# Two batches of modulation and VectorE-only lower halves in a two-block transformer kernel

## The chip, the cores and the metric

The kernel runs on one core of one Trainium2 chip. The metric is the device time of one execution in microseconds; lower is better. The engines are named as the profile names them: PE (TensorE matmul) and PEld (its weight loads), DVE (VectorE), ACT (ScalarE), POOL (GpSimd) and SP (the queue that issues most DMAs).

## The reference, cut to what matters

Two transformer blocks follow each other on a sequence of 1024 tokens of width 1024, all in float32:

```python
def first_block(x, ...):
    h = rms_norm(x, norm_mix);  x = x + gated_deltanet(h, ...)      # 8 heads of 128
    x = x + squared_relu_mlp(rms_norm(x, norm_mlp), w_up, w_down)   # 1024 -> 4096 -> 1024
    return rms_norm(x, norm_final)

def second_block(x, c, ctx, c_ctx, w_mod, b_mod, ...):
    mx = split(silu(c) @ w_mod + b_mod, 6)          # six vectors of 1024
    mc = split(silu(c_ctx) @ w_mod + b_mod, 6)      # only the first two are used
    hx = modulate(rmsnorm(x, g_norm1), mx[0], mx[1])
    hc = modulate(rmsnorm(ctx, g_norm1), mc[0], mc[1])
    ...                                             # attention and gated linear attention
    x = x + mx[2] * (mixed @ w_out)
    x = x + mx[5] * swiglu(modulate(rmsnorm(x, g_norm2), mx[3], mx[4]), w_gu, w_down)
    return rmsnorm(x, g_final)
```

The modulation, `silu(c) @ w_mod`, is a product of one vector with a 1024 x 6144 matrix. It depends on none of the tokens, so it may be computed at any time before the second block's norms.

## The kernel before, in words

**Split operands.** Every large matrix product is done in three TensorE passes over rounded parts: an operand is copied to an upper half (`hi`, by ACT) and the rest is its lower half (`lo = raw - hi`, a subtraction with two inputs in SBUF). `wload` (L125 to L141) loads a weight tile, lets ACT make `whi` (L139) and either DVE or POOL make `wlo` (L140). In the DeltaNet stage POOL makes it for three of the four projections of each head (L274, L552: 24 tiles of 128x1024), DVE for the others.

**Stages, in the order of the trace.** (1) DeltaNet, in four pairs of heads. `project` (L272) does a 128x512 product per half of the tokens, then a causal convolution on DVE (L288 and three times L290), then a Silu on ACT (L292). Beside it DVE inverts triangular blocks row by row (L396, L400). (2) The output projection of heads 0 to 5 (L659 to L667): eight column blocks `o`, two halves of tokens each, 18 matmuls per half. A result leaves PSUM by DVE in the first half and by ACT in the second (L667). (3) `Up.half` and `Up.operands`: the residual (x transposed by PE, from tiles `xin2` that `out_tile` loads at L731), heads 6 and 7, the norm and the operands of the next stage. (4) The first MLP's `Up`: a Strassen scheme with seven products of 12 matmuls for each of 16 blocks `f`, 112 products; `evac` takes results from PSUM (L754), `spill` (from L1838) writes seven operand tiles per block to memory. (5) `Down`: four groups of 3, 4, 4 and 3 of those blocks, 28 products each. At a change of group seven sets of tiles `T` are loaded again and split by `Down.split` (L1893): ACT makes the upper half (L1898), DVE the lower half of every even tile and POOL that of every odd one (L1899). `prepare` makes weight sums on POOL (L1925 to L1930) and splits the block (L1934 on ACT, L1935 on DVE); a product's result is added to x on DVE (L1957). (6) A last group, the mixer of the second block and its output. (7) The second MLP in the same form: `Up` with 22 blocks, `Down` with three groups of 3 (its additions are L1959).

**The modulation.** `Modulation.stream` is a generator. It loads 128x512 tiles of `w_mod` (L873), multiplies each with one silu value per partition and adds it up on DVE (L884 for the first of eight tiles, L886 for the rest), then transposes and reduces the sum (L893, L895). There are twelve groups of eight tiles; groups 0 to 3 are done for two vectors, the others for one. `Modulation.finish` adds the rest up with four small PE products. Before the change groups 3 to 11 run in `Up`, one step after each product (`up.hook`, L775), with loads on SP's queue into the halves of x that are free there; groups 0 to 2 run in `Down`, one step after every second product from the 15th on (L799 to L801), with loads on POOL's queue.

**Order.** Each engine works through its own queue in order, and each DMA queue too. The program is written in Python order, but a scheduler places the instructions on each engine by the readiness that it expects, so the order on an engine need not be that of the text. Buffers of a pool tag are handed out again when their last reader is done; a new pool on memory of a closed one waits for the closed one's last readers.

Of the kernel before, what the change touches and what calls it, by code (L numbers as in the profile page):

```python
# [9 lines left out]
F32 = mybir.dt.float32  # L10
# [195 lines left out]
def deltanet(k, spill, dbg=None):  # L206

    nc, tc, A = k.nc, k.tc, k.A
    with ExitStack() as ctx:
# [62 lines left out]
        def project(h, part, out):  # L272

            W = k.wload(w_in[:, part * 1024 + h * 128: part * 1024 + h * 128 + 128], lo=nc.gpsimd if part != 1 else None)  # L274
# [276 lines left out]
        def gates(h, pr):  # L551
            W = k.wload(w_in[:, 3072 + h * 128:3072 + h * 128 + 128], lo=nc.gpsimd)  # L552
# [105 lines left out]

        x = []  # L659
# [8 lines left out]
        return gated, x  # L668
# [45 lines left out]
def dn_out_and_mlp(k, gated, mod, norms, cpd, x2d, ud, td):  # L714

    nc, A = k.nc, k.A
    x = k.x
    with ExitStack() as ctx:
# [47 lines left out]
        mod.open(P)  # L766
        ms = mod.stream(list(range(3, 12)), [x[f][:, 512:1024] for f in range(8)], nc.sync)
# [7 lines left out]
        up.hook = lambda: next(ms, None)  # L775
# [5 lines left out]
        ms = mod.stream(list(range(3)), [k.e() for _ in range(5)], nc.gpsimd)  # L781
# [11 lines left out]
        def hook(done, left):  # L793
            if left == 10:
                drain(ms)
                mod.finish()
# [50 lines left out]
class Modulation:  # L847
# [3 lines left out]
    def __init__(self, k):  # L851
# [5 lines left out]
        self.bm = k.vec["b_mod_2"]  # L857

    def open(self, P):
        nc, sc = self.k.nc, self.sc  # L860
        self.R = P.tile([128, 64, 4], F32, name="modR")
        nc.scalar.activation(sc[:, 0, :], self.k.vec["c_2"], AF.Silu)
        nc.scalar.activation(sc[:, 1, :], self.k.vec["c_ctx_2"], AF.Silu)

    def stream(self, groups, raws, q):
# [11 lines left out]
        for n, (g, j) in enumerate(todo):  # L877
            vs = range(2 if g < 4 else 1)
            if j == 0:
                accs = [k.e() for _ in vs]  # L880
# [9 lines left out]
            if j == 7:  # L890
                for v in vs:
                    tr = k.e()
                    nc.vector.transpose(tr, accs[v])  # L893
                    m = 48 * v + 4 * g
# [4 lines left out]
    def finish(self):  # L899

        k, nc, bm = self.k, self.k.nc, self.bm
        ps = k.pt((128, 64))
# [3 lines left out]
        nc.vector.tensor_tensor(out=k.mod, in0=ps[:, 0:48], in1=bm, op=ALU.add)  # L906
        nc.vector.tensor_tensor(out=k.modc, in0=ps[:, 48:64], in1=bm[:, 0:16], op=ALU.add)
# [712 lines left out]
class Up:  # L1620
# [112 lines left out]
    def run(self, upto=None):  # L1733

        while self.done < (upto or len(self.seq)):
# [126 lines left out]
class Down:  # L1862
# [267 lines left out]
def whole(ctx, tc, A, out):  # L2130
# [11 lines left out]
    with ExitStack() as c2:  # L2142
        k.xp = c2.enter_context(tc.tile_pool(name="xp", bufs=1, reuse_waits="tile"))
        k.s1 = c2.enter_context(tc.tile_pool(name="s1", bufs=16, reuse_waits="tile"))
        gated, k.x = deltanet(k, spill)
# [31 lines left out]
```

## Time and profile before

| what | us |
|---|---|
| median of three runs (lowest, highest) | 3005.15 (3001.58, 3014.09) |
| the profiled execution's own time | 3009.24 |
| its span from the first to the last instruction | 3007.2 |
| PE busy | 2804.1 (93%) |
| DVE busy | 2110.5 (70%) |
| ACT busy | 1404.8 (47%) |
| POOL busy | 799.6 (27%) |
| mean granted clock of PE | 0.978 |

PE is busy for nine tenths of the span, so what is lost are the stretches in which it waits and those after a wait in which it was granted the lower of its two clock levels. A share of busy time over the whole span tells little here; the stages differ, and each is read by itself.

### The profile page before, as it was taken

To read this page: it belongs to the slowest core of one execution; us is meant where nothing else is said; L and a number is where in the kernel's file an instruction comes from. 1 tells how busy PE (TensorE), PEld (TensorE's weight loads), DVE (VectorE), ACT (ScalarE), POOL (GpSimd) and SP (SyncE) were. 2 spreads that over 40 slices of the span, in tenths; PEclk is the share of its full clock that TensorE was granted. 3 is DMA by queue.
4 is the path that set the end of the run, shared out by engine and by line. 5 is a ranking of instruction groups with operands and counts; after the bars stand their busy time and mean duration, and the time that the engine had idled before them with its cause. 6 is when DMAs were issued, how large, how long until landed. Compare 5 with 4: busy or idle time off the path is not lost. (4 is left out here: it accounts for less than half of the span.)

```text
span 3007.2 us, 43812 instructions
## 1 busy us (share of the span) xinstructions
PE 2804.1 (93%) x16336; PEld 2284.9 (76%) x16336; DVE 2110.5 (70%) x3254; ACT 1404.8 (47%) x2685; POOL 799.6 (27%) x665
## 2 busy tenths in 40 slices
PE   7899989999899988899899998999899999999998
PEld 5777778787687867787777777788777788887777
DVE  5868686855988779877856667677757755556784
ACT  6343535333555553335633334677645433334345
POOL 1102020102133365542422222121120322334432
PEclk9999999999999999999999999999999999999999
DMA  4313131232577665442621111001033433335433
GB/s 110 58 28 73 27 81 31 58 120 99 162 236 230 204 227 177 141 139 73 185 68 41 48 50 45 12 29 60 15 126 106 133 102 100 97 115 173 132 105 109
DMA packets 330084, 310.16 MB, mean 103 GB/s; under 512 B 36640, under 2 KB 254720, under 8 KB 329872
## 3 DMA queue, kind: packets, MB, share of 16 engines
q1 hardware_dynamic: 277088, 220.90, 24.0%
q10 hardware_dynamic: 46480, 65.46, 6.0%
q0 software_dynamic: 6304, 21.01, 3.1%
q8 instruction: 128, 2.10, 0.3%
q14 instruction: 84, 0.69, 0.1%
HBM read 232.83 MB, written 74.48 MB: 102 GB/s over the span
## 5 line engine op out<-in xcount | busy, mean ns | idle before, releaser
L1709 PE MATMUL pt<-T,blk 128*128 128x512 f32 x608 | 244.8, 404 | 16.2 <-DVE e L754 8.4
L1711 PE MATMUL pt<-T,blk 128*128 128x512 f32 x608 | 244.7, 403 | 5.4 <-DVE blk L1698 5.4
L1710 PE MATMUL pt<-T,blk 128*128 128x512 f32 x608 | 244.5, 402 | 0.7 <-DVE T L1786 0.6
L139 ACT CAST whi<-wraw 128x1024 fp32r<-128x1024 f32 (+3 forms) x126 | 116.0, 920 | 221.9 <-PE pg L150 180.1
L149 PE MATMUL pg<-dhi,whi 128*128 128x512 f32 (+1 forms) x528 | 213.5, 404 | 2.1 <-ACT pre L285 1.8
L151 PE MATMUL pg<-dhi,wlo 128*128 128x512 f32 (+1 forms) x528 | 212.5, 402 | 1.5 <-POOL wlo L140 1.5
L150 PE MATMUL pg<-dlo,whi 128*128 128x512 f32 (+1 forms) x528 | 212.1, 402 | 1.1 <-DVE dlo L188 1.0
L1950 PE MATMUL pt<-T,blk 128*128 128x512 f32 x368 | 150.2, 408 | 29.4 <-DVE x L1957 19.7
L149 PE MATMUL pg<-xhi,whi 128*128 128x512 f32 x416 | 170.8, 410 | 1.4 <-ACT e L1024 1.4
L151 PE MATMUL pg<-xhi,wlo 128*128 128x512 f32 x416 | 167.4, 402 | 0.3 <-DVE wlo L140 0.3
L150 PE MATMUL pg<-xlo,whi 128*128 128x512 f32 x416 | 167.1, 402 | 0.0
L140 DVE TENSOR_TENSOR wlo<-wraw,whi 128x1024 fp32r<-128x1024 f32 (+3 forms) x101 | 110.0, 1090 | 74.6 <-ACT whi L139 69.8
L1709 PEld LDWEIGHTS pt<-T,blk 128*128 128x128 f32 x608 | 116.8, 193 | 48.1 <-ACT blk L1697 7.0
L1952 PE MATMUL pt<-T,blk 128*128 128x512 f32 x368 | 148.2, 403 | 1.4 <-DVE blk L1935 1.4
L1951 PE MATMUL pt<-T,blk 128*128 128x512 f32 x368 | 148.4, 403 | 0.0
L1711 PEld LDWEIGHTS pt<-T,blk 128*128 128x128 f32 x608 | 117.3, 193 | 33.6 <-DVE blk L1698 6.3
L1698 DVE TENSOR_TENSOR blk<-xb,blk 128x512 fp32r<-128x512 f32 x121 | 102.9, 851 | 54.9 <-ACT blk L1697 53.0
L1351 DVE TENSOR_TENSOR pl<-pt,ph 128x512 fp32r<-128x512 f32 x160 | 106.3, 683 | 47.2 <-ACT ph L1346 46.5
L1710 PEld LDWEIGHTS pt<-T,blk 128*128 128x128 f32 x608 | 117.1, 193 | 28.9 <-DVE T L1786 1.9
L1898 ACT CAST T<-T 128x512 fp32r<-128x512 f32 x161 | 96.1, 618 | 89.0 <-DMA T<-td 44.2
L1934 ACT CAST blk<-T 128x384 fp32r<-128x384 f32 (+1 forms) x133 | 71.8, 540 | 138.2 <-PE pt L1952 83.1
L1697 ACT CAST blk<-xb 128x512 fp32r<-128x512 f32 x121 | 74.2, 621 | 116.3 <-PE pt L1711 46.9
(570 smaller groups left out, 8273.2 us busy)
## 6 DMA issues: line engine op xcount, KB each, us to landing
x<-w_mod SPq DMA_DIRECT2D x72, 256.0 KB
wraw<-w_in SPq DMA_DIRECT2D x35, 512.0 KB
T<-td SPq DMA_DIRECT2D x69, 256.0 KB
wraw<-dn_w_in SPq DMA_DIRECT2D x32, 512.0 KB
td<-e ACTq DMA_DIRECT2D x55, 256.0 KB
xb<-w_gu SPq DMA_DIRECT2D x44, 256.0 KB
wraw<-w_gu SPq DMA_DIRECT2D x22, 512.0 KB
xin<-x SPq DMA_DIRECT2D x16, 512.0 KB
```

The lines of the kernel that those rows point to most:

```text
L139: nc.scalar.copy(hi, raw)
L140: (lo or nc.vector).tensor_tensor(out=lo_t, in0=raw, in1=hi, op=ALU.subtract)
L149: nc.tensor.matmul(out, hi[:, w, :], Hhi[k][:, sl], start=first and k == 0, stop=False)
L150: nc.tensor.matmul(out, hi[:, w, :], Hlo[k][:, sl], start=False, stop=False)
L151: nc.tensor.matmul(out, lo[:, w, :], Hhi[k][:, sl], start=False, stop=last and k == n - 1)
L1351: nc.vector.tensor_tensor(out=pl, in0=ps, in1=ph, op=ALU.subtract)
L1709: nc.tensor.matmul(ps, w[:, 0, j], T[j][:, 0], start=not c and j == 0, stop=False, skip_group_check=c)
L1710: nc.tensor.matmul(ps, w[:, 0, j], T[j][:, 1], start=False, stop=False, skip_group_check=c)
L1711: nc.tensor.matmul(ps, w[:, 1, j], T[j][:, 0], start=False, stop=j == 3, skip_group_check=c)
L1950: nc.tensor.matmul(ps, w[:, 0, j], T[j][:, 0], start=not c and j == 0, stop=False, skip_group_check=c)
L1951: nc.tensor.matmul(ps, w[:, 0, j], T[j][:, 1], start=False, stop=False, skip_group_check=c)
L1952: nc.tensor.matmul(ps, w[:, 1, j], T[j][:, 0], start=False, stop=j == n - 1, skip_group_check=c)
```

## The change

1. The `lo` argument that sent 24 lower halves of DeltaNet weights to POOL goes; DVE makes all of them.
2. The modulation is split in two. Groups 0 to 2 are streamed between the products of DeltaNet's output projection, two steps after each half, from buffers of DeltaNet's own pool (tags `k` and `dec`) with loads on POOL's queue, and get a `finish` of their own at the end of that stage. The vectors that they need are loaded ahead of that stage, on ACT's queue instead of SP's. Groups 3 to 11 stay in `Up`, but start after 24 products. Nothing of the modulation is left in `Down`.
3. `Down.split` has DVE make every lower half, in both MLPs.
4. In `Up.run` a product's result is taken from PSUM before `Down.start` is called, not after.

```diff
 def project(h, part, out):
-            W = k.wload(w_in[:, part * 1024 + h * 128: ...], lo=nc.gpsimd if part != 1 else None)
+            W = k.wload(w_in[:, part * 1024 + h * 128: ...])
 def gates(h, pr):
-            W = k.wload(w_in[:, 3072 + h * 128:3072 + h * 128 + 128], lo=nc.gpsimd)
+            W = k.wload(w_in[:, 3072 + h * 128:3072 + h * 128 + 128])
 # deltanet, output projection
+        k.load_vecs(VECS[1:], nc.scalar)
+        mod = Modulation(k)
+        mod.open(P, [0, 1, 2])
+        raws = [P.tile([128, 2, 512], F32, tag="k", name=k.nm("mraw"), bufs=4) for _ in range(4)]
...
+                t = P.tile([128, 2, 512], F32, tag="dec", name=k.nm("macc"), bufs=2)
...
+        ms = mod.stream([0, 1, 2], [t[:, j] for t in raws for j in range(2)], nc.gpsimd, tmp)
         for o in range(8):
...
                 (nc.scalar.copy if i else nc.vector.tensor_copy)(x[o][:, sl], ps)
+                next(ms, None)
+                next(ms, None)
+        drain(ms)
+        mod.finish()
 # dn_out_and_mlp
-        up.hook = lambda: next(ms, None)
+        up.hook = lambda: next(ms, None) if up.done > 24 else None
...
         drain(chain(ms, back(HALVES[0])))
-        ms = mod.stream(list(range(3)), [k.e() for _ in range(5)], nc.gpsimd)
+        mod.finish()
...
             if left == 10:
-                drain(ms)
-                mod.finish()
                 u.append(last_group(k, s1, "s1", ud[28:32]))
...
-            elif left > 10:
-                if done > 14 and done % 2 == 0:
-                    next(ms, None)
-            else:
+            elif left < 10:
 # Up.run
             r = self.product(f, m)
+            if r:
+                self.evac(f, *r)
             if f == self.n - 1 and self.after:
                 self.after(m)
-            if r:
-                self.evac(f, *r)
 # Down.split
-            (nc.gpsimd if j % 2 else nc.vector).tensor_tensor(out=t[:, 1], in0=t[:, 1].bitcast(F32), in1=t[:, 0], op=ALU.subtract)
+            nc.vector.tensor_tensor(out=t[:, 1], in0=t[:, 1].bitcast(F32), in1=t[:, 0], op=ALU.subtract)
```

How it moves instructions, at three places. **DVE in the output projection** (`x<-pg` takes a result of column block o from PSUM, `wlo` is the lower half of a later block's weights, `macc` and `modR` belong to the modulation). Before, from the end of the scan on:

```order
L140 TENSOR_TENSOR wlo_6251<-wraw_6249,whi_6250 128x768
L549 TENSOR_TENSOR ol_5826<-z_5680,oh_5825 128x512
L667 COPY x_6201<-pg_6208 128x512
L140 TENSOR_TENSOR wlo_6298<-wraw_6296,whi_6297 128x768
L667 COPY x_6248<-pg_6255 128x512
L140 TENSOR_TENSOR wlo_6345<-wraw_6343,whi_6344 128x768
L667 COPY x_6295<-pg_6302 128x512
```

With the change, in the same place; the last row here is the lower half for block 4, and the row `wlo_6323` for block 3 stands five rows above the first one:

```order
L900 SCALAR_TENSOR_TENSOR macc_6166<-mraw_6130,sc,macc_6166 128x512 x4
L680 COPY x_6258<-pg_6265 128x512
L907 STREAM_TRANSPOSE macc_6285<-macc_6166 128x512 x2
L909 TENSOR_REDUCE modR_6126<-macc_6285 128x16 x2
L898 TENSOR_SCALAR macc_6290<-mraw_6127,sc 128x512 x2
L900 SCALAR_TENSOR_TENSOR macc_6290<-mraw_6127,sc,macc_6290 128x512 x2
L900 SCALAR_TENSOR_TENSOR macc_6290<-mraw_6128,sc,macc_6290 128x512 x2
L680 COPY x_6320<-pg_6327 128x512
L900 SCALAR_TENSOR_TENSOR macc_6290<-mraw_6128,sc,macc_6290 128x512 x2
L900 SCALAR_TENSOR_TENSOR macc_6290<-mraw_6129,sc,macc_6290 128x512 x4
L900 SCALAR_TENSOR_TENSOR macc_6290<-mraw_6130,sc,macc_6290 128x512 x2
L140 TENSOR_TENSOR wlo_6382<-wraw_6380,whi_6381 128x768
```

Between `wlo_6323` and `wlo_6382` there now stand 34 instructions of the modulation and two copies; before, one copy stood between two lower halves.

**SP's queue at the end of the output projection** (`xin` are the x tiles of the residual, `dn_w_out` and `mlp_w_up` weights; in brackets the semaphores that a load waits for, `DMASW` being those of POOL's loads). Before:

```order
L138 DMA wraw_6296<-dn_w_out 128x6x128 [waits DMAHW3_49,DVE_49]
L731 DMA xin_1224_6536<-x 128x1024 [waits PE_49]
L138 DMA wraw_6343<-dn_w_out 128x6x128 [waits DMAHW4_49,DVE_49]
L731 DMA xin_1225_6538<-x 128x1024 [waits PE_49]
L731 DMA xin_1226_6540<-x 128x1024
L731 DMA xin_1227_6542<-x 128x1024
L731 DMA xin_1248_6687<-x 128x1024
L138 DMA wraw_6390<-dn_w_out 128x6x128 [waits DMAHW5_49,DVE_49]
```

With the change:

```order
L138 DMA wraw_6611<-dn_w_out 128x2x512 [waits DMAHW0_49,DVE_49]
L138 DMA wraw_6617<-dn_w_out 128x2x512 [waits DMAHW1_49,DVE_49]
L1680 DMA wraw_6893<-mlp_w_up 128x8x128 [waits DMAHW2_49,DVE_49]
L748 DMA xin_1236_6640<-x 128x1024 [waits DMASW6_49,DMASW5_49,DMASW7_49,DMASW0_49,PE_49]
L748 DMA xin_1237_6642<-x 128x1024 [waits PE_49]
L748 DMA xin_1238_6644<-x 128x1024
L748 DMA xin_1239_6646<-x 128x1024
```

The x tiles lie on memory that the modulation now uses to the end of the stage. They moved behind all weights of the output projection and the first weight of `Up`; the first waits for the modulation's last loads, and the PE count that the second waits for is raised by the four products of `finish`, which stand behind the last product of the projection.

**DVE in the first MLP's `Down`**, shortly after its start (`x<-x,ps` adds a product to x, `blk` is a weight block's lower half, `T` a tile's lower half, L884 and L886 modulation). Before:

```order
L1957 TENSOR_TENSOR x_6154<-x_6154,ps_9595 128x512
L1935 TENSOR_TENSOR blk_9607<-T_6529,blk_9607 128x384
L884 TENSOR_SCALAR e_9787<-e_9525,sc 128x512
L884 TENSOR_SCALAR e_9788<-e_9525,sc 128x512
L1957 TENSOR_TENSOR x_6248<-x_6248,ps_9611 128x512
L1935 TENSOR_TENSOR blk_9623<-draw_9334,blk_9623 128x384
L886 SCALAR_TENSOR_TENSOR e_9787<-e_9526,sc,e_9787 128x512
L886 SCALAR_TENSOR_TENSOR e_9788<-e_9526,sc,e_9788 128x512
```

With the change:

```order
L1972 TENSOR_TENSOR x_6258<-x_6258,pg_9684 128x512
L1950 TENSOR_TENSOR blk_9696<-T_6632,blk_9696 128x384
L1914 TENSOR_TENSOR T_7045<-T_7045 128x512
L1972 TENSOR_TENSOR x_6199<-x_6199,ps_9699 128x512
L1914 TENSOR_TENSOR T_7046<-T_7046 128x512
L1950 TENSOR_TENSOR blk_9711<-T_6633,blk_9711 128x384
L1914 TENSOR_TENSOR T_6630<-T_6630 128x512
L1972 TENSOR_TENSOR x_6320<-x_6320,ps_9715 128x512
```

The modulation's instructions are gone from between the additions, and every tile's lower half (odd and even numbers) stands on DVE.

## Rows read from the trace of the kernel before

**Rows 1.** The page, part 1: busy time and share of the span.
```profile
PE 2804.1 (93%) x16336; PEld 2284.9 (76%) x16336; DVE 2110.5 (70%) x3254; ACT 1404.8 (47%) x2685; POOL 799.6 (27%) x665
```

**Rows 2.** Stretches, us; busy us (count) per engine; granted clock; DMA share; GB/s.
```profile
70.00:620.00 550.00, 507.39 (x3556) 421.59 (x3554) 412.35 (x882) 247.84 (x662) 71.72 (x64) 0.98 0.24 53
620.00:703.00 83.00, 82.97 (x435) 70.02 (x434) 34.13 (x72) 23.16 (x57) 0.00 (x0) 1.00 0.28 94
...
1062.00:1091.00 29.00, 25.64 (x104) 20.16 (x102) 15.13 (x21) 20.05 (x39) 16.15 (x17) 0.94 0.99 345
1091.00:1235.00 144.00, 127.78 (x526) 100.78 (x525) 138.84 (x181) 51.09 (x94) 75.83 (x65) 0.96 0.50 161
1235.00:1395.00 160.00, 153.73 (x669) 123.40 (x667) 121.36 (x171) 66.74 (x122) 67.83 (x49) 0.98 0.36 120
2345.00:2735.00 390.00, 390.00 (x1681) 316.87 (x1681) 215.22 (x280) 140.39 (x240) 125.40 (x90) 1.00 0.34 111
2735.00:2942.00 207.00, 193.57 (x814) 155.69 (x813) 163.22 (x222) 83.31 (x156) 82.83 (x67) 0.98 0.40 130
```

**Rows 3.** PE's waits, 1091 to 1395 us: total, times, longest (us).
```profile
PE pt L1950 <- DVE x L1957: 19.7, 6, 6.0
```

**Rows 4.** Timeline of PE: the longest of those waits, at a change of group.
```profile
1248.69 0.76 PE L1950 MATMUL pt<-T,blk 128*128 128x512 f32 x1 [6.01 <-DVE x L1957]
```

**Rows 5.** DVE by form, 1060 to 1400 us: count, busy, mean ns, idle.
```profile
L1899 DVE TENSOR_TENSOR T<-T 128x512 fp32r<-128x512 f32 x56 | 59.2, 1067 | 16.9 <-ACT T L1898 16.9
...
L886 DVE SCALAR_TENSOR_TENSOR e<-e,sc,e 128x512 f32<-128x512 f32 x42 | 37.8, 927 | 0.0
```

**Rows 6.** Single lines, duration ns min/median/max: splits (both MLPs), modulation, additions.
```profile
L1899 DVE TENSOR_TENSOR T<-T x98: 644/692/1814, 1067.0 to 2887.7; 128x512 fp32r<-128x512 f32 x98
...
L1899 POOL TENSOR_TENSOR T<-T x63: 1262/1601/1862, 1067.7 to 2887.3; 128x512 fp32r<-128x512 f32 x63
...
L886 DVE SCALAR_TENSOR_TENSOR e<-e,sc,e x42: 736/740/1784, 1109.7 to 1217.0; 128x512 f32<-128x512 f32 x42
...
L1957 DVE TENSOR_TENSOR x<-x,pt x64: 643/675/689, 1091.2 to 1394.6; 128x512 f32<-128x512 f32 x64
```

**Rows 7.** Timeline of DVE and of POOL at the same change of group.
```profile
1239.44 3.49 DVE L1899 TENSOR_TENSOR T<-T 128x512 fp32r<-128x512 f32 x2
...
1238.93 1.75 POOL L1899 TENSOR_TENSOR T<-T 128x512 fp32r<-128x512 f32 x1
```

**Rows 8.** PE's waits, 785 to 1062 us (the first Up).
```profile
PE pt L1709 <- DVE e L754: 6.0, 2, 5.9
```

**Rows 9.** The stretch right after that long wait; columns as in rows 2.
```profile
807.00:816.00 9.00, 9.00 (x29) 7.16 (x30) 9.00 (x14) 4.14 (x8) 3.58 (x2) 0.71 0.78 262
```

**Rows 10.** PE's longest waits in DeltaNet, 70 to 620 us.
```profile
PE pt L468 <- ACT qT L292: 22.6, 9, 4.7
```

**Rows 11.** DeltaNet: POOL's lower halves by form; a DVE record beside one at 279.2.
```profile
L140 POOL TENSOR_TENSOR wlo<-wraw,whi 128x1024 fp32r<-128x1024 f32 x23 | 56.2, 2445 | 107.7 <-ACT whi L139 80.5 <-PE ps L524 16.9 <-PE pg L151 10.3
...
279.74 2.14 DVE L396 TENSOR_TENSOR pm<-X,A 64x252 f32<-64x252 f32 x1
```

**Rows 12.** DVE's groups by form, 620 to 703 us (output projection).
```profile
L667 DVE COPY x<-pg 128x512 f32<-128x512 f32 x8 | 5.5, 692 | 19.6 <-PE pg L151 19.6
...
L140 DVE TENSOR_TENSOR wlo<-wraw,whi 128x1024 fp32r<-128x1024 f32 x2 | 2.4, 1221 | 3.5 <-PE pg L151 3.5
```

**Rows 13.** Timeline: SP's first residual load; ACT on the kernel's first x tiles.
```profile
642.13 0.34 SPq L731 DMA_DIRECT2D xin<-x  x1
...
4.99 1.06 ACT L175 ACTIVATE xj<-xin 128x1024 f32<-128x1024 f32 x1 [0.81 <-DMA xin<-x]
...
7.99 1.06 ACT L175 ACTIVATE xj<-xin 128x1024 f32<-128x1024 f32 x1 [0.46 <-DMA xin<-x]
```

**Rows 14.** PE's waits, 2735 to 2942 us (second Up's end, second Down).
```profile
PE pt L1950 <- DVE xb L1959: 9.6, 2, 5.0
PE pt L1709 <- DVE e L2036: 3.7, 1, 3.7
```

More of the change, by code (lines that the diff above doesn't have):

```diff
@@ L272, in project @@
         def project(h, part, out):
-            W = k.wload(w_in[:, part * 1024 + h * 128: part * 1024 + h * 128 + 128], lo=nc.gpsimd if part != 1 else None)
+            W = k.wload(w_in[:, part * 1024 + h * 128: part * 1024 + h * 128 + 128])
             n = part * 8 + h
@@ L657, in deltanet, with tmp @@
                 values(p + 1)
+        k.load_vecs(VECS[1:], nc.scalar)
+        mod = Modulation(k)
+        mod.open(P, [0, 1, 2])
+        raws = [P.tile([128, 2, 512], F32, tag="k", name=k.nm("mraw"), bufs=4) for _ in range(4)]
+        tmps = []
+        def tmp():
+            if not tmps:
+                t = P.tile([128, 2, 512], F32, tag="dec", name=k.nm("macc"), bufs=2)
+                tmps.extend((t[:, 0], t[:, 1]))
+            return tmps.pop(0)
+        ms = mod.stream([0, 1, 2], [t[:, j] for t in raws for j in range(2)], nc.gpsimd, tmp)
         x = []
@@ L667, in deltanet @@
                 (nc.scalar.copy if i else nc.vector.tensor_copy)(x[o][:, sl], ps)
-        return gated, x
+                next(ms, None)
+                next(ms, None)
+        drain(ms)
+        mod.finish()
+        return gated, x, mod
 HALVES = [slice(0, 512), slice(512, 1024)]
@@ L765, in dn_out_and_mlp @@
         up.operands(out_tile)
-        mod.open(P)
-        ms = mod.stream(list(range(3, 12)), [x[f][:, 512:1024] for f in range(8)], nc.sync)
+        mod.open(P, list(range(3, 12)))
+        ms = mod.stream(list(range(3, 12)), [x[f][:, 512:1024] for f in range(8)], nc.sync, k.e)
         def back(h):
@@ L857, in __init__, with open, stream @@
         self.bm = k.vec["b_mod_2"]
[L859 to L865, printed above, removed]
+        nc.scalar.activation(sc[:, 0, :], k.vec["c_2"], AF.Silu)
+        nc.scalar.activation(sc[:, 1, :], k.vec["c_ctx_2"], AF.Silu)
+    def open(self, P, groups):
+        self.g0, self.n = 4 * groups[0], 4 * len(groups)
+        self.nx = max(0, 16 - self.g0) if groups[-1] > 3 else self.n
+        self.R = P.tile([128, self.n + self.nx, 4], F32, name=self.k.nm("modR"))
+    def stream(self, groups, raws, q, tmp):
         k, nc, sc = self.k, self.k.nc, self.sc
@@ L879, in stream @@
             if j == 0:
-                accs = [k.e() for _ in vs]
+                accs = [tmp() for _ in vs]
             src = raws[n % len(raws)]
@@ L891, in stream @@
                 for v in vs:
-                    tr = k.e()
+                    tr = tmp()
                     nc.vector.transpose(tr, accs[v])
-                    m = 48 * v + 4 * g
+                    m = self.n * v + 4 * g - self.g0
                     nc.vector.tensor_reduce(out=self.R[:, m:m + 4, :].rearrange("p c r -> p (c r)"),
@@ L901, in finish @@
         k, nc, bm = self.k, self.k.nc, self.bm
-        ps = k.pt((128, 64))
+        g, n, nx = self.g0, self.n, self.nx
+        ps = k.pt((128, n + nx))
         for r in range(4):
@@ L905, in finish @@
                              tile_position=(0, 32 * r))
-        nc.vector.tensor_tensor(out=k.mod, in0=ps[:, 0:48], in1=bm, op=ALU.add)
-        nc.vector.tensor_tensor(out=k.modc, in0=ps[:, 48:64], in1=bm[:, 0:16], op=ALU.add)
+        nc.vector.tensor_tensor(out=k.mod[:, g:g + n], in0=ps[:, 0:n], in1=bm[:, g:g + n], op=ALU.add)
+        nc.vector.tensor_tensor(out=k.modc[:, g:g + nx], in0=ps[:, n:n + nx], in1=bm[:, g:g + nx], op=ALU.add)
 def affine(k, g, shift, scale, name):
@@ L2144, in whole @@
         k.s1 = c2.enter_context(tc.tile_pool(name="s1", bufs=16, reuse_waits="tile"))
-        gated, k.x = deltanet(k, spill)
-        k.load_vecs(VECS[1:], nc.sync)
-        mod = Modulation(k)
+        gated, k.x, mod = deltanet(k, spill)
         norms = FirstNorms(k, x1d)
```

## The prediction

> **What bounds the kernel now.** I read the page's shares first: PE is busy for 2804.1 of 3007.2 us [rows 1], so a gain must come out of the 203 us in which it is not, or out of work done at the lower clock. Then I read the stretches that the change touches [rows 2], and in each what PE waits for. A pace without loss is needed: in 2345 to 2735 PE does 1681 matmuls in 390 us, 0.232 us each, at a granted clock of 1.00.
>
> The first Down is the worst of them. From 1091 to 1235 there are 526 matmuls, 122.0 us at that pace, in 144: 22.0 lost. DVE is busy for 138.84 of the 144, so it is the bound there. From 1235 to 1395 there are 669, 155.2 in 160: 4.8 lost, with DVE at 121.36 of 160 [rows 2]. The list of PE's waits names the same engine: PE waits for a PSUM tile until DVE has added the product before to x, 19.7 us in six waits [rows 3]. The longest, 6.01 us, is at a change of group [rows 4]. The rest of the 26.8 is work at the lower of the clock's levels, 1.2 against 2.4 GHz: the granted clock is 0.96 and 0.98 [rows 2].
>
> The first Up has one such wait, 5.9 us on DVE taking a product out of PSUM [rows 8], and the 9 us after it have a granted clock of 0.71, with 29 matmuls [rows 9], 6.7 us at the pace above. So this place costs 5.9 + 2.3 = 8.2 us. DeltaNet waits for Silu's qT, 22.6 us in nine [rows 10]. In the output projection PE is never idle: 82.97 of 83, with DVE at 34.13 [rows 2]. The second Down and the end of Up before it lose 9.6 + 3.7 us in three waits [rows 14].
>
> The sum goes against the profiled execution, 3009.24 us with a span of 3007.2. That is 4.1 above the median of the three runs, 3005.15, which I take off at the end.
>
> **DeltaNet (edit 1): −4.** POOL's lower halves of 128x1024 take 2445 ns each [rows 11]; DVE's take 1221 ns [rows 12]. So 24 x 1.22 = 29 us go to DVE, which has 412 of 550 busy [rows 2]: room for them. POOL's took 56.2 us, and beside one a DVE operation on 64x252 took 2.14 us [rows 11], though with a quarter of the columns of a lower half it should need about 0.3: the halves hold DVE up. The same delay stands ahead of four of the nine waits for qT, some 1.7 us each, 7 us. Against this, a lower half now stands among the convolution's instructions, 1.22 us on that chain in some heads; I take 3 us of it. Bounds: −10 (all the delays go, and no new one) and +10 (eight heads at 1.22).
>
> **Output projection (edit 2): +7.** This is the place shown in the order of DVE. Between the lower halves of blocks 3 and 4 stand 34 modulation instructions and two copies. An accumulation takes 740 ns in the median [rows 6], a copy 692 [rows 12]: 34 x 0.74 + 2 x 0.69 = 26.5 us. PE has two blocks meanwhile, 4 x 18 = 72 matmuls, 16.7 us. So block 4's lower half is up to 9.8 us late; the products of upper halves, one third to two thirds of a block, can go first, and part of the modulation may be done in DVE's slack before (49 of 83 us are idle). I take 7, with 0 (the slack holds it) and 14 (the late start also costs 4 us at the lower clock) as bounds.
>
> **The residual's loads (edit 2): +5.** They start at 642.13 now [rows 13], 60 us before their use. Afterwards the second one waits for four products of `finish` that stand behind the projection, so they are issued when PE is about to need them. The nearest rows are the kernel's start: the same kind of tile lands for ACT at 4.99 and two tiles later at 7.99 [rows 13], 1.5 us a tile. The third and fourth then come some 5 to 7 us after the issue, and a few transposes and products stand ahead. Bounds +2 and +9.
>
> **First Up (edits 2, 4): −8 and +4.** With no modulation in the first 24 products, what DVE had queued ahead of that evacuation is gone, and the 8.2 us with it; −8.5 and 0 are the bounds, the latter if another instruction stands there. At its other end the stream now runs to about product 106 of 112 instead of 88, so the eight x loads (2.1 MB, 6 us at 345 GB/s) come later, into 1062 to 1091, where the DMA share is 0.99 [rows 2]. The loads of groups 0 to 2, 6 MB in the first Down, no longer follow. I take +4, between 0 and +8. Taking the result before `Down.start` costs and brings nothing: the scheduler's order hardly moves there.
>
> **First Down (edits 2, 3): −19.** Removed from DVE: 37.8 us of accumulations [rows 5] and 18 other modulation instructions at 0.74, together 51. Added: 42 lower halves at 0.69, 29. Given back: the 56 that DVE has already take 59.2 us [rows 5], 20.6 over 56 x 0.69. The spread is 644 to 1814 ns for an operation with two inputs in SBUF, but 643 to 689 for the addition that reads PSUM [rows 6]; at the change of group two took 3.49 us while POOL worked with 1.75 us each [rows 7]. POOL's weight sums stay, so I give back half, 10. DVE then has about 228 instead of 260 us over both stretches, and in the first one, where all the modulation was, about 100 instead of 138.84: no bound any more. The changes of group remain: half of the 6.01 us, and about 5 elsewhere, 8 of 26.8 lost. Bounds −8 and −26.
>
> Here a rule speaks against the change. The Trainium skill's "Perfetto Trace Analysis", section "Optimizing Scalar/DVE Operations", says that where DVE is saturated, giving some of its work to another engine, GpSimd even, may make sense, though the two share a port and it then might not help. The trace sides with its second half [rows 7], by which the sum is as above; by the first half this term would be about −10, and the next one +8.
>
> **Second Down: −3.** 21 lower halves, 14.5 us, go to DVE, at 163.22 of 207 [rows 2]; what POOL's held up is given back. The two waits of 9.6 us [rows 14] are at changes of group too, so I expect a third less there. Bounds −8 and +8.
>
> **At nothing:** the vectors' loads on ACT's queue (ahead of a stage without waits), 24 weight loads on POOL's queue (POOL has 0.00 busy in 620 to 703 [rows 2]), and the second `finish`, two DVE additions in Up's last products.
>
> Sum: −4 + 7 + 5 − 8 + 4 − 19 − 3 = −18, so 2991.2 in the profiled execution, and 2987 for the median.
>
> **Rivals.**
> (a) *Down keeps its changes of group.* The six waits [rows 3] are as much ends of loads and splits as modulation. For it: the longest, 6.01 us [rows 4], comes when modulation is over. Against it: DVE at 138.84 of 144. Then Down gives −8 instead of −19: 2998.
> (b) *DVE stays the bound.* The lower halves take DVE as long as they take POOL's half away, and nothing is given back since weight sums keep POOL busy: 51 − 29 = 22 us less instead of 32, and all of it bunched at the changes of group. For it: 75.83 and 67.83 us of POOL in the two stretches [rows 2]; against it, the 3.49 us [rows 7]. Down −10, second Down +8: 20 more, 3007. This is the first half of the rule above.
> (c) *Slower: the lower halves stand on DeltaNet's chain.* DVE has one queue; each of 24 now stands before instructions of the convolution that qT needs, while POOL did them beside it. The price is 24 x 1.22 = 29 instead of −4, 33 more: 3020. It decides if more than about 15 of the 24 lengthen a wait for qT (−18 + 4 + 15 x 1.22 is about +4). For it: order of DVE in one chain; against it, 138 idle us of DVE and only nine waits now [rows 10].
> (d) *The holds of POOL cost more than I see.* DeltaNet −10 and Down −26: 13 more, 2974, and lower if the second Down gives −8.
>
> **How the numbers follow.** About 0.5%, 15 us, is what a measurement of this kernel can tell from no change: 2990.1 and 3020.2 are the bounds. Chances: the forecast .44, with an own range of 2978 to 2996; (a) .18; (b) .12; (c) .14, from 3008 to 3034; (d) .12. Faster: two thirds of the forecast (.29), all of (d) (.12), and a third of (a) (.06), .47. Slower: two thirds of (c), .09, and a little of (b) with the upper bounds of projection and loads: .11. The rest, .42, is within. The range from 2965 to 3019 leaves out half of (c) and a third of (d), and leaves a tenth for bounds that add up.
>
> **What would show it.** Right: in the 300 us of the first Down PE's waits on the addition to x fall from 19.7 to below 9, DVE's splits come near 0.69 in the mean, and its busy time there falls by 30; the 5.9 us in Up and the 0.71 after it are gone. A new wait of PE of 5 to 10 us stands before block 4 of the projection, on a lower half, and one of 3 to 7 at its end, on the residual's tiles. Wrong: splits still at 1 us in the mean (then (b)); waits of Down on additions that stay near 15 (then (a)); more or longer waits for qT, with DVE above 440 of 550 (then (c)). The forecast as a whole falls if projection and residual together cost more than 23 us, or if the first Up's wait comes back at product 25.

## The result

The change takes 2973.66 us in the median of six runs (2967.39 to 2978.34), the kernel before 3004.39 (six runs): a ratio of 0.989, 95% interval 0.9871 to 0.9909. In a later comparison it was 2968.59 against 3003.64, 0.9871 (0.9851 to 0.9891). It is faster, by 31 us where 18 were forecast, and inside the range.

The profiled execution of the change (2967.41) lies 6.3 us below its median, that of before 4.9 above, so the two traces are 41.8 us apart and not 31. The page's first part, after:

```profile
PE 2790.5 (94%) x16344; PEld 2275.9 (77%) x16344; DVE 2088.1 (70%) x3343; ACT 1409.0 (48%) x2690; POOL 644.8 (22%) x578
```

POOL is 155 us less busy than in [rows 1] and DVE, which took that work over, is 22 us less busy too. The stretches of [rows 2], at the places that they have now (columns as there; the third lies inside the second, the fourth follows Up's first products, and neither has a counterpart there):

```profile
70.00:606.00 536.00, 510.43 (x3589) 424.25 (x3588) 396.73 (x913) 255.42 (x673) 17.63 (x45) 0.97 0.25 57
606.00:694.00 88.00, 79.29 (x393) 64.87 (x392) 67.11 (x125) 20.35 (x49) 10.77 (x20) 0.96 0.34 107
640.00:680.00 40.00, 32.55 (x132) 25.78 (x131) 38.99 (x61) 5.28 (x8) 6.99 (x13) 0.91 0.43 130
790.00:820.00 30.00, 28.63 (x124) 22.69 (x123) 23.06 (x26) 15.72 (x29) 12.63 (x8) 1.00 0.61 195
1060.00:1089.00 29.00, 25.40 (x115) 19.84 (x114) 22.08 (x37) 21.47 (x40) 9.96 (x13) 1.00 0.98 345
1089.00:1208.00 119.00, 117.46 (x508) 95.01 (x507) 93.17 (x142) 51.85 (x95) 32.96 (x25) 1.00 0.45 146
1208.00:1368.00 160.00, 156.00 (x673) 125.84 (x672) 120.71 (x180) 65.43 (x119) 41.36 (x32) 0.99 0.36 118
2705.00:2901.00 196.00, 189.78 (x810) 152.61 (x809) 156.47 (x240) 82.03 (x155) 54.43 (x46) 0.99 0.41 135
```

In the first Down PE is now busy for 117.46 of 119 us at a granted clock of 1.00, with DVE at 93.17 where it was 138.84 of 144. The output projection got worse: 79.29 of 88, and in the 40 us from 640 on DVE is the bound (38.99 of 40) and the clock 0.91. PE's waits in the change that answer to those of before or are new, in DeltaNet (first three lines), projection and residual (three), first Up (one), first Down (two stretches, one each), end of the second Up and second Down (two); line, waited for, us, times, longest:

```profile
PE pg L151 <- DVE wlo L140: 10.0, 3, 3.3
PE pt L376 <- DVE N L377: 6.1, 3, 2.6
PE pt L468 <- ACT qT L292: 0.6, 2, 0.3
...
PE pg L151 <- DVE wlo L140: 5.1, 1, 5.1
PE pg L149 <- ACT x L680: 3.5, 3, 1.2
PE pg L754 <- DMA xin<-x: 1.8, 2, 1.2
...
PE pt L1724 <- DVE e L771: 4.6, 3, 1.9
...
PE pt L1965 <- DVE x L1972: 1.4, 1, 1.4
...
PE pt L1965 <- DVE x L1972: 4.0, 3, 2.2
...
PE pt L1724 <- DVE e L2051: 2.9, 1, 2.9
PE pt L1965 <- DVE xb L1974: 2.9, 2, 1.8
```

The 22.6 us on qT [rows 10] are 0.6, the 19.7 on x [rows 3] are 1.4 + 4.0, the 9.6 and 3.7 of the second Down [rows 14] are 2.9 and 2.9. New are 5.1 us on a lower half in the projection and 1.8 on x tiles. The splits of Down on DVE, in the first Down by form and in both as one line:

```profile
L1914 DVE TENSOR_TENSOR T<-T 128x512 fp32r<-128x512 f32 x98 | 81.3, 852 | 16.7 <-ACT T L1913 16.6
...
L1914 DVE TENSOR_TENSOR T<-T x161: 672/684/1785, 1064.2 to 2850.7; 128x512 fp32r<-128x512 f32 x161
```

98 splits take 81.3 us where 56 took 59.2 [rows 5]: 42 more cost 22 us. The mean fell from 1067 to 852 ns, not to 690, since POOL's weight sums are still there: each of the 19 splits that take over 900 ns runs beside one of them.

The traces can be laid beside each other stage by stage, by the ends of the same instruction in each: the third copy of the projection out of PSUM (P), the first, seventh and last evacuation of the first Up (U1, U7, U48), the last addition of the first Down (D), the first and last of the second Down (E1, E84). Column one is the length before in us, the others the difference to it:

| stage | before | change | change again | edit 1 | edit 3 | edits 2, 4 |
|---|---|---|---|---|---|---|
| start to P | 645.6 | -12.3 | -5.8 | -25.5 | +0.3 | +5.0 |
| P to U1 | 111.3 | +12.2 | +12.4 | +0.2 | 0.0 | +11.7 |
| U1 to U7 | 60.8 | -9.2 | -9.2 | +1.2 | -0.7 | -9.6 |
| U7 to U48 | 267.6 | +8.4 | +7.9 | -0.7 | +2.4 | +8.5 |
| U48 to D | 309.9 | -25.9 | -25.9 | -0.6 | -12.9 | -24.3 |
| D to E1 | 1361.6 | -5.3 | -3.3 | -3.2 | -2.2 | -4.6 |
| E1 to E84 | 185.3 | -9.2 | -5.9 | +1.0 | -7.1 | -1.0 |

The row of DeltaNet (start to P) scatters most: 6.5 us between the two traces of the change. The second Down differs by 3.3 us between them, and P to U1 is +8.4 and +8.5 in two later runs that alter the change only in later stages. D to E1, the middle of the kernel, is shorter than before in every run, also in those whose edits lie elsewhere, so there the one execution of before had lost some us more. The columns to the right belong to the experiments.

### The profile page after: what moved, and what is told of

Read it like the earlier page. It is cut to its first block, busy times and chain, and to the rows that moved or that the text cites. A ratio compares the mean times of both kernels' runs of the same rounds, so it can differ in the third digit from the quotient of the medians.

```text
span 2965.4 us, 43793 instructions
## 1 busy us (share of the span) xinstructions
PE 2790.5 (94%) x16344; PEld 2275.9 (77%) x16344; DVE 2088.1 (70%) x3343; ACT 1409.0 (48%) x2690; POOL 644.8 (22%) x578
## 5 line engine op out<-in xcount | busy, mean ns | idle before, releaser
L1724 PE MATMUL pt<-T,blk 128*128 128x512 f32 x608 | 242.1, 400 | 12.1 <-DVE e L771 4.6
L1726 PE MATMUL pt<-T,blk 128*128 128x512 f32 x608 | 241.9, 398 | 5.4 <-DVE blk L1713 5.4
L1725 PE MATMUL pt<-T,blk 128*128 128x512 f32 x608 | 241.8, 398 | 0.7 <-DVE T L1801 0.6
L140 DVE TENSOR_TENSOR wlo<-wraw,whi 128x1024 fp32r<-128x1024 f32 (+3 forms) x125 | 138.9, 1111 | 69.5 <-ACT whi L139 67.8
L1965 PE MATMUL pt<-T,blk 128*128 128x512 f32 x368 | 146.6, 398 | 8.5 <-DVE x L1972 5.4
L1967 PE MATMUL pt<-T,blk 128*128 128x512 f32 x368 | 145.6, 396 | 0.0
L1966 PE MATMUL pt<-T,blk 128*128 128x512 f32 x368 | 145.5, 395 | 0.0
L1914 DVE TENSOR_TENSOR T<-T 128x512 fp32r<-128x512 f32 x161 | 129.9, 831 | 20.4 <-ACT T L1913 20.3
L1713 DVE TENSOR_TENSOR blk<-xb,blk 128x512 fp32r<-128x512 f32 x121 | 102.4, 847 | 56.9 <-ACT blk L1712 55.2
L1724 PE MATMUL ps<-T,blk 128*128 128x512 f32 x304 | 121.3, 402 | 8.8 <-ACT e L1729 4.7
```

Of the source, the lines that this page charges most:

```text
L140: (lo or nc.vector).tensor_tensor(out=lo_t, in0=raw, in1=hi, op=ALU.subtract)
L1724: nc.tensor.matmul(ps, w[:, 0, j], T[j][:, 0], start=not c and j == 0, stop=False, skip_group_check=c)
L1725: nc.tensor.matmul(ps, w[:, 0, j], T[j][:, 1], start=False, stop=False, skip_group_check=c)
L1726: nc.tensor.matmul(ps, w[:, 1, j], T[j][:, 0], start=False, stop=j == 3, skip_group_check=c)
L1914: nc.vector.tensor_tensor(out=t[:, 1], in0=t[:, 1].bitcast(F32), in1=t[:, 0], op=ALU.subtract)
L1965: nc.tensor.matmul(ps, w[:, 0, j], T[j][:, 0], start=not c and j == 0, stop=False, skip_group_check=c)
```

## The experiments

A hold is a DVE operation that takes longer than its kind because POOL works beside it. To measure holds, each operation's duration above the lower quartile of its own line and shape is added up over a stage; these sums are called DVE's durations above the quartile. In DeltaNet before they are 44 us, 41 of them in operations beside one of POOL's lower halves, and 3.5 us in the change. The theory after the result (A): POOL's work on SBUF holds up DVE's, in DeltaNet far more than the prediction counted, and lets go of it when the lower halves leave POOL. Rivals: the halves help because they are ready sooner, or by a new order (D); the parts need each other (C); a saturated engine should not get work back (B).

**Edit 1 alone.** The diff is that of edit 1 on the kernel before.

```diff
-W = k.wload(w_in[:, part * 1024 + h * 128: ...], lo=nc.gpsimd if part != 1 else None)
+W = k.wload(w_in[:, part * 1024 + h * 128: ...])
```

> The kernel before with edit 1 alone: DVE makes the 24 DeltaNet lower halves, all else stays. Theory A (holds): while POOL works, DVE's operations with two inputs in SBUF are held up; the 24 halves of POOL cost DVE about 41 us over DeltaNet (44 us of durations above the quartile before, 3 after), more than the 29 us that DVE takes over, and PE gets part of it. Then DeltaNet up to the second block of the projection is 10 to 18 us shorter, as in the change (12.3), the rest as before: about 2990. Rival C (the parts need each other): edit 1 alone brings under 5 us, about 3000 or more.

Measured: 2983.65 us, ratio 0.9932 (0.9913 to 0.9951), 22 us less in the medians, all in DeltaNet (-25.5 to P in its trace). PE's wait for qT in DeltaNet, 22.6 us before [rows 10], is nearly gone:

```profile
PE pt L468 <- ACT qT L292: 0.4, 2, 0.3
```

C falls for this part.

**Edit 3 alone.**

```diff
-(nc.gpsimd if j % 2 else nc.vector).tensor_tensor(out=t[:, 1], ...)
+nc.vector.tensor_tensor(out=t[:, 1], ...)
```

> The kernel before with edit 3 alone: DVE makes every lower half of the intermediate tiles, the modulation stays in Down. Theory A (holds): DVE takes 63 x 0.69 = 43 us over and gets back about 45 us (30 in the first Down, 15 in the second); DVE's busy time in the first Down stays within 5 us of before, the first Down is 0 to 8 us shorter, the second 6 to 10; sum 6 to 16 shorter, about 2993. Rival B (work of a saturated engine should go to another one): DVE is at 138.84 of 144 us in the first Down, so taking work back there lengthens it by 5 to 15 us and the second gains nothing: 3009 or more.

Measured: 2985.73, ratio 0.9933 (0.9919 to 0.9947), 20 us less; 12.9 of it in the first Down, more than A had it, and 7.1 in the second. B falls: the first Down in two stretches (columns as in rows 2),

```profile
1092.00:1224.00 132.00, 123.87 (x515) 99.27 (x514) 124.42 (x188) 51.41 (x93) 48.88 (x49) 0.96 0.56 180
1224.00:1384.00 160.00, 154.59 (x674) 124.92 (x673) 131.38 (x199) 66.63 (x120) 43.36 (x32) 0.98 0.37 117
```

has 124.42 + 131.38 us of DVE, against 138.84 + 121.36 before: DVE does 42 operations more in 4 us less.

**Edits 2 and 4 alone** (the change with edits 1 and 3 undone; the diff is theirs).

```diff
-W = k.wload(w_in[:, part * 1024 + h * 128: ...])
+W = k.wload(w_in[:, part * 1024 + h * 128: ...], lo=nc.gpsimd if part != 1 else None)
...
-nc.vector.tensor_tensor(out=t[:, 1], ...)
+(nc.gpsimd if j % 2 else nc.vector).tensor_tensor(out=t[:, 1], ...)
```

> The change with edits 1 and 3 undone: only the modulation is moved (and the evacuation order). Theory A (holds): the first Down gains half of the change's 24 to 26 us, 10 to 15, from 51 us less on DVE; projection and residual lose 12 as in the change; first Up 0 to -2: about 3003, no difference. Rival C (the modulation alone made Down slow): Down gains 20 or more, and the sum is -8 to -14: about 2993.

Measured: 2994.23, ratio 0.9965 (0.9952 to 0.9978), 11 us less. Here A was wrong and C right: the modulation's leaving alone takes 24.3 us from the first Down. The edit pays 11.7 from P to U1 and 5.0 ahead of P. The three parts are 22, 20 and 11 us in the medians, together 53 where the change has 31 to 35: edits 2 and 3 remove the same loss in Down (24.3 and 12.9, together 25.9), because there are only 26.8 us to lose. The first Down in two stretches (columns as in rows 2):

```profile
1106.00:1226.00 120.00, 116.47 (x496) 93.82 (x495) 92.11 (x119) 51.18 (x93) 61.55 (x44) 0.99 0.42 133
1226.00:1386.00 160.00, 158.35 (x690) 127.98 (x689) 122.18 (x167) 68.32 (x123) 68.81 (x49) 1.00 0.39 127
```

DVE is busy for 92.11 + 122.18 = 214.3 us with 42 of the 98 tiles' lower halves on POOL, and for 213.9 in the change, where all are DVE's. The 42 cost no busy time, since other operations get shorter: the lower halves of blocks (L1950) take 93.7 us here and 76.3 in the change.

**Work on POOL that nobody waits for.**

```diff
 (lo or nc.vector).tensor_tensor(out=lo_t, in0=raw, in1=hi, op=ALU.subtract)
+if beside is not None:
+    for n in (hi[:, 0:4].bitcast(F32), hi[:, 4:8].bitcast(F32)):
+        nc.gpsimd.tensor_tensor(out=beside, in0=n, in1=n, op=ALU.subtract)
```

> The change, with POOL given work beside DVE in DeltaNet that nobody waits for: for each of the 24 weights POOL subtracts the upper half from itself into a scratch tile, two operations of 128x512, about 2.5 us together. The lower halves themselves stay on DVE, and no result is different. Theory A (holds): DVE's durations above the quartile in DeltaNet rise from 3 to 35 or more us, and DeltaNet gets 10 to 20 us longer than in the change: about 2987. Rival D (what helps is that DVE's lower half takes 1.22 us instead of 2.45 and comes sooner, or the new order of instructions): POOL's idle work costs under 3 us: about 2975.

Measured: 2996.32, ratio to before 0.9965 (0.9951 to 0.9978), 23 to 28 us slower than the change, more than A has. DVE's durations above the quartile rose to 30, not 35. Start to P is 13.9 us longer than before, so 26 and 20 longer than in the two traces of the change. PE's wait for qT is back; in its trace (all lines are three or four further down), that wait and POOL's added work, 70 to 632 us:

```profile
PE pt L472 <- ACT qT L296: 14.6, 7, 3.2
...
L143 POOL TENSOR_TENSOR pj<-whi 128x512 f32<-128x512 f32 x48 | 65.2, 1357 | 106.0 <-ACT whi L139 103.6
```

D falls: here the lower halves are DVE's work as in the change, and up to the last Silu DVE (943 instructions) and ACT (702) do the same in the same order as there. (POOL's queue also holds the fills of 128x4 that pad the convolution's input; ACT's waits ahead of that input, in before and here, name PE or a DMA, one of 6.8 us in before nothing that the profile shows, and never POOL. Nor does ACT wait for POOL ahead of an upper half, which POOL's added work reads.) How a hold looks, from the timeline of the kernel before, and below it the first operation of the convolution in before and in the change (least, median, most ns):

```profile
82.86 2.38 POOL L140 TENSOR_TENSOR wlo<-wraw,whi 128x1024 fp32r<-128x1024 f32 x1 [3.52 <-PE pg L151]
83.50 2.02 DVE L288 TENSOR_SCALAR acc<-pre,convw 128x512 f32<-128x512 f32 x1 [4.42 <-ACT pre L285]
```

```profile
L288 DVE TENSOR_SCALAR acc<-pre,convw x48: 469/485/2674, 44.3 to 575.8; 128x512 f32<-128x512 f32 x48
```

```profile
L288 DVE TENSOR_SCALAR acc<-pre,convw x48: 468/476/489, 44.6 to 559.5; 128x512 f32<-128x512 f32 x48
```

DVE's operation starts 0.64 us after POOL's, ends 0.28 us after it, and takes 2.02 us instead of 0.48. With the lower halves off POOL none of the 48 takes over 0.49. The Trainium skill's "SBUF — State Buffer", section "Who interferes with whom", says that the two engines share one port pair, which one instruction holds to its end; the rows agree, since DVE's operation ends only behind POOL's.

**Edits 1 and 3 without the move of the modulation** (the two diffs above, on the kernel before).

```diff
+W = k.wload(w_in[:, part * 1024 + h * 128: ...])
...
+nc.vector.tensor_tensor(out=t[:, 1], ...)
```

> The kernel before with edits 1 and 3 and without the move of the modulation. Each alone was about 20 us faster, and they lie in different stages. Theory A (holds): the two add up, 38 to 42 us faster than before, about 2965, and so faster than the whole change, whose early batch of modulation costs some 17 us in the projection and the residual and gains less in Down once the lower halves are on DVE. Rival C (the early batch is needed for the gain): about 2974 or more.

Measured: 2964.41, ratio 0.9869 (0.9854 to 0.9884), 39.5 us less: they add up, as A has it. So the two small edits do at least as much as the whole change (0.9869 against 0.989 and 0.9871).

**A slower modulation in Down.** On the kernel with edits 1 and 3:

```diff
-if done > 14 and done % 2 == 0:
+if done > 14 and done % 3 == 0:
```

> As the run with edits 1 and 3, and in the first Down a modulation step follows every third product from the 15th on instead of every second. With edit 3 alone the first Down still lost some 15 of its 26 us. Theory E (it is the density of modulation on DVE): 4 to 10 us less in the first Down than with edits 1 and 3 alone, about 2958. Rival (a) of the prediction (the rest is changes of group): within 3 us of it.

Measured: 2971.26, ratio 0.9888 (0.9873 to 0.9903). The first Down is 13.0 us shorter than before where the run with edits 1 and 3 has 15.0, within 3 us of it as rival (a) has it. But the run says little on E, since the edit hardly spread the modulation: its 48 multiplications on DVE start between 8.8 and 163.6 us after U48 in the run with edits 1 and 3, and between 8.5 and 175.0 here. PE's waits for additions are 10.9 us in four there, 12.2 in five here. The longest stands in both where it stood before [rows 4], at a change of group (first row: edits 1 and 3, second: this run):

```profile
1214.70 0.51 PE L1950 MATMUL pt<-T,blk 128*128 128x512 f32 x1 [4.69 <-DVE x L1957]
```

```profile
1217.05 0.77 PE L1950 MATMUL pt<-T,blk 128*128 128x512 f32 x1 [5.35 <-DVE x L1957]
```

With edits 2 and 4 alone the wait at that place is 1.26 us. So it needs the modulation beside the change of group; how much spreading would bring stays open. The rest of the 7 us between the medians lies mostly in D to E1, which neither touches (-0.5 against -6.4).

**Modulation from Up's first product.**

```diff
-up.hook = lambda: next(ms, None) if up.done > 24 else None
+up.hook = lambda: next(ms, None)
```

> The change with the second batch of modulation begun at Up's first product again instead of the 25th. If the wait of 5.9 us at the first evacuations came from the modulation there (as the prediction has it), Up is 7 to 9 us longer at its sixth evacuation, and what the change lost over the rest of Up, about 8 us, is not lost: about 2974, no difference. Rival: the late loss has another cause (then 2982), or the early wait has (then 2966).

Measured: 2966.5, ratio 0.9874 (0.9857 to 0.989), the same as the change. U1 to U7 is +0.4 instead of -9.2, U7 to U48 is 0.0 instead of +8.4. The early wait is back, 5.94 us where the change has 1.20 (first row: this run, second: the change):

```profile
799.06 0.76 PE L1724 MATMUL pt<-T,blk 128*128 128x512 f32 x1 [5.94 <-DVE e L771]
```

```profile
802.04 0.47 PE L1724 MATMUL pt<-T,blk 128*128 128x512 f32 x1 [1.20 <-DVE e L771]
```

So the later start of the second batch moves a loss of 8 to 9 us from the beginning of Up to its rest, and gains nothing.

**Edit 4 undone** (the evacuation after `Down.start` again).

```diff
-if r:
-    self.evac(f, *r)
 if f == self.n - 1 and self.after:
     self.after(m)
+if r:
+    self.evac(f, *r)
```

> The change with edit 4 undone: a product's result is taken from PSUM after the start of Down's loads again. The prediction costed edit 4 at nothing since the order hardly moves: within 3 us of the change. Rival: the 3 to 4 us wait of PE on an evacuation at the end of the second Up, 2.9 in the change, is back above 3.5 and the kernel 3 to 6 us slower.

Measured: 2963.16, ratio 0.9869 (0.9852 to 0.9885), against 0.9871 for the change beside it: no difference, and PE's wait on the evacuation is 3.1 us. Edit 4 is worth nothing that can be measured.

**The change again.** No edit.

> The change itself once more, as the yardstick on the same chip for the three others, and for a second trace of it: 2967 to 2978 as before. The first trace had a lower granted clock after two waits of some 3 us in DeltaNet (0.87 and 0.91) where the run with edit 1 alone kept 1.00 after the same waits and was 7 us ahead there. If that is chance, this trace's DeltaNet differs from the first one's by some us with the same waits; if it belongs to the change, it is the same.

Measured: 2968.59 (2958.58 to 2979.14). Its traced DeltaNet is 6.5 us longer to P than the first one's, with the same waits on lower halves, N and X. It was chance: see the last section.

**Two mends in the projection, together and one by one.**

```diff
+ahead = wout(0)
 for o in range(8):
-    W = k.wload(A["dn_w_out"][0:768, o * 128:o * 128 + 128], nk=6)
+    W = ahead
+    if o < 7:
+        ahead = wout(o + 1)
     for i, sl in enumerate(HALVES):
...
         next(ms, None)
         next(ms, None)
-drain(ms)
-mod.finish()
+        if (o, i) == (6, 1):
+            drain(ms)
+            mod.finish()
```

`wout(o)` is the `wload` of block o. The first mend is the `ahead` part, the second the finish after block 6.

> The whole change with two mends in the output projection: the weights of a block are asked for one block ahead, so that fewer modulation instructions stand before a lower half (22 instead of 34 between two of them), and the first batch is finished ahead of the last block, which puts the loads of the residual's tiles ahead of a weight of Up. Theory F (the early batch costs 17 us by these two waits): 6 to 12 us less than the change, about 2965. Rival G (its cost is the clock after any wait there and DVE's load, which stay): within 3 us of the change, about 2973.

> The change with the first mend alone: the projection's weights asked for one block ahead. By the same reckoning 9 to 13 us less than the change: the wait of 5.1 us on a lower half is gone, the residual's tiles still come late (its first product waits 2 us or more).

> The change with the second of the two mends alone: the first batch of modulation is finished ahead of the last block of the output projection, so that the residual's x tiles are loaded earlier. If each wait costs what stands beside it (about 11 us in the projection by the late lower half and the clock after it, 6 at the residual's start), this gives 5 to 8 us less than the change, and the wait of 5 us on a lower half stays. If one mend alone carried the 23 us by which both together beat the change, it gives 0 or 20.

Measured: both 2950.31, ratio 0.9822 (0.9808 to 0.9837), the fastest kernel of this study, 23 and 18 us under the two medians of the change, where F has 6 to 12; weights ahead 2959.13, 0.9857 (0.9838 to 0.9877); early finish 2965.42, 0.9876 (0.9856 to 0.9897).

A part of the 23 is DeltaNet, which the mends do not touch. The 46th of its 48 Silus is the same instruction in all kernels with edit 1; of the 14.9 us between the traces of the change and of both mends 8.4 lie before it. Against the change with edit 4 undone, whose trace is as long up to there (544.8 and 544.7 us), both mends are 10.8 us shorter, 8.5 of it between that Silu and U1. So F has about the right size, and G falls. By stretches: from that Silu to the projection's last copy out of PSUM the change takes 141.3 us, with the weights ahead 134.1, with both 134.6. From that copy to U1 the change takes 62.4 and 62.6 in its two traces, 58.6 and 58.8 in the two runs above that alter it only later (modulation from Up's first product, edit 4 undone), with the early finish 55.2, with both 57.0. The weights ahead so give 7 us and the early finish 3 to 7, and PE's wait on a late lower half and its wait for x tiles are gone, each with its mend. SP's loads of the x tiles in the change, and with both mends (start, us, engine, line):

```profile
687.08 0.37 SPq L1680 DMA_DIRECT2D wraw<-mlp_w_up  x1
687.62 9.05 SPq L748 DMA_DIRECT2D xin<-x  x8
```

```profile
669.02 6.98 SPq L756 DMA_DIRECT2D xin<-x  x8
677.45 2.95 SPq L1688 DMA_DIRECT2D wraw<-mlp_w_up  x2
```

They start 18.6 us earlier, 10.2 of it when counted from the 46th Silu, and ahead of Up's weights. In medians the early finish alone brings 3 to 8 us (its six runs lie between 2958.81 and 2975.11), with DeltaNet's scatter over it.

## Why the prediction was right, and where it was wrong

The side, the range and the order of the parts held: first Down the largest gain, projection and residual the price. The likeliest case (2978 to 2996) did not hold the time; it came out at rival (d)'s 2974, and for half of (d)'s reason: POOL's holds did cost more than was counted. That the number is (d)'s to the microsecond is luck, since DeltaNet and the second Down gave more than (d) has, and projection and residual cost more.

- **DeltaNet, -4.** The step that failed. "The same delay stands ahead of four of the nine waits for qT, some 1.7 us each, 7 us": I priced four holds that I had seen, while POOL's 56.2 us [rows 11] hold DVE up all through the stage, and a chain of convolutions then carries each delay on. DVE's durations above their quartile were 44 us in this stage, and 3.5 in the change. Edit 1 alone is worth 22 us in the medians, and the wait for qT went from 22.6 to 0.6. In the ten traces with edit 1 and no added work on POOL the 46th Silu comes 7 to 22 us earlier than before, 16 in the mean; in the three with POOL's halves it comes at 563.9 to 566.9 us. The lower bound of -10 did not hold that: it should have been the 22.6 us of all waits for qT [rows 10]. Rival (c), lower halves on the chain, is there but small: PE has 10.0 us in three waits on lower halves that it did not have, less than what went.
- **Output projection and residual, +7 and +5.** The mechanism was right, the size of the first term too small. From the 46th Silu to the projection's last copy out of PSUM the change takes 141.3 us, the run with edit 1 alone 129.6: 11.7, not 7. From there to U1 it is 62.4 and 55.5: 6.9 in place of 5, and 3.1 and 3.3 in the two runs that alter the change only later. Together that is 18.6, or 15 in those two, not 12. The x tiles cost PE a wait of 1.8 us, where 3 to 7 were asked. The late lower half is there, 5.1 us forecast as 7 (9.8 at most), in the order that the prediction gave: on DVE, from block 3's lower half at 634.69 to block 4's at 657.94, and PE behind it:

```profile
634.69 0.95 DVE L140 TENSOR_TENSOR wlo<-wraw,whi 128x768 fp32r<-128x768 f32 x1
635.56 0.88 DVE L898 TENSOR_SCALAR macc<-mraw,sc 128x512 f32<-128x512 f32 x2
636.35 9.36 DVE L900 SCALAR_TENSOR_TENSOR macc<-mraw,sc,macc 128x512 f32<-128x512 f32 x14
645.63 0.68 DVE L680 COPY x<-pg 128x512 f32<-128x512 f32 x1
...
652.64 5.38 DVE L900 SCALAR_TENSOR_TENSOR macc<-mraw,sc,macc 128x512 f32<-128x512 f32 x8
657.94 0.95 DVE L140 TENSOR_TENSOR wlo<-wraw,whi 128x768 fp32r<-128x768 f32 x1
```

```profile
658.94 0.80 PE L151 MATMUL pg<-ohi,wlo 128*128 128x512 f32 x1 [5.09 <-DVE wlo L140]
```

  What was left out: DVE's copies out of PSUM come late too (one at 632.63 behind the end of the scan, the one at 645.63 behind the modulation), PE waits three times for ACT's copies, 3.5 us, and its granted clock is 0.91 in the 40 us from 640. The run with both mends still takes 191.6 us from that Silu to U1, 6.5 over edit 1 alone; 5.0 of it lie before the projection's last copy, where the three waits still stand. What the rest is made of was not tried.
- **First Up, -8 and +4.** -9.2 and +8.4. The first term was right. The second stood for a burst of loads at Up's end, but only 2.8 us of the loss lie there, after the 36th of 48 evacuations. 5.4 lie between the 7th and the 15th, where the modulation now begins and a wait on an evacuation comes back, at 862.5, of 1.47 us. The run without the late start shows that the two terms belong together.
- **First Down, -19.** -25.9, at the bound of -26. DVE fell by 46 us, not 32, to 213.9 over the two stretches, and PE's waits on additions to 5.4 us, where "below 9" was asked. The sum kept 8 us of loss at the changes of group and elsewhere; now PE is busy for 273.5 of the 279 us, and the longest wait at a change of group is 2.2. Rival (a) had chance .18 and is out: the modulation's leaving alone takes 24.3, with POOL's halves still there.
- **Second Down, -3.** -9.2 and -5.9 in the two traces of the change, -5.1 to -9.2 in all eleven with edit 3, where -8 was the lower bound. Rival (b) is out: in the second Down and, with edit 3 alone, in the first DVE got work back and was less busy after it, in the first where it had 138.84 of 144 us. So the first half of the rule of the Trainium skill's "Perfetto Trace Analysis", section "Optimizing Scalar/DVE Operations", does not hold for these subtractions.
- **At nothing.** Edit 4 was nothing. Of the other edits costed at nothing none was tried alone.

The gains were too small for two reasons: in DeltaNet the holds, and in the first Down the loss kept at the changes of group, which the modulation's leaving alone removes. The price in the projection and the residual was too small as well, by 3 to 7, and that hid part of it.

## What to carry to other kernels

Before giving work to POOL, or leaving it there, add up how much longer DVE's operations take than their own kind's lower quartile. Where that came near or above the time that DVE needs for the work itself (in DeltaNet 44 against 29 us, in the first Down 20.6 against 29), DVE was better off doing it alone, even where it was the busiest engine. That is two stages of one kernel. Work that is moved into a stage with idle DVE time still queues on DVE ahead of short, urgent instructions: ask for what PE needs a block ahead before the long work is put in. Parts of a change that mend the same stall do not add up; measuring each alone, and the pair without the third, tells which of them pays.

## What was not expected

The same wait leaves different clocks. In DeltaNet PE waits for X from memory, 3.44 us in the first trace of the change and 3.27 with edit 1 alone, at the same place in the same order of instructions; the ten microseconds from 290 on are at a granted clock of 0.76 in the one and 1.00 in the other (of each kernel the wait, and that stretch; columns of the second row as in rows 2):

```profile
286.11 0.31 PE L426 MATMUL ps<-X,N 32*32 32x32 f32 x2 [3.44 <-DMA X<-Xd]
...
290.00:300.00 10.00, 10.00 (x223) 7.45 (x218) 2.11 (x6) 3.07 (x8) 0.00 (x0) 0.76 0.18 50
```

```profile
285.70 0.24 PE L426 MATMUL ps<-X,N 32*32 32x32 f32 x2 [3.27 <-DMA X<-Xd]
...
290.00:300.00 10.00, 10.00 (x236) 7.75 (x234) 4.00 (x11) 3.31 (x8) 0.00 (x0) 1.00 0.15 44
```

The length of the wait does not decide it: in the second trace of the change it is 3.00 us, and the ten microseconds from 290 are at 0.77. The same happens 150 us later. What decides it no run here shows. Up to the 46th Silu the two traces of the change are 553.1 and 559.5 us long, the change with edit 4 undone 544.8: 14.7 us between executions whose DeltaNet has the same instructions. That is half of what the change gains, so a stage is compared by stretches without such a wait, or over several executions.
